# A two-layer Conformer trunk: reading a half bank twice, adding saved sums early, and storing the last tile in halves

## The chip, the cores and the metric

One core of a Trainium2 chip runs the whole program in one launch. The metric is the device time of an execution in microseconds, as the median of several runs.

## What is computed

`x` has 512 positions of 1024 features, in float32. Two layers follow one another, and each has two feed-forward blocks around a mixer:

```python
for l in range(DEPTH):          # DEPTH = 2
    x = x + 0.5 * swiglu(rms_norm(x, ffn1_norm[l]), gate1[l], up1[l], down1[l])
    x = x + mixer(rms_norm(x, mix_norm[l]))      # convolution group and differential attention
    x = x + 0.5 * swiglu(rms_norm(x, ffn2_norm[l]), gate2[l], up2[l], down2[l])

def swiglu(h, w_gate, w_up, w_down):             # 1024 -> 2816 -> 1024
    return (silu(h @ w_gate) * (h @ w_up)) @ w_down
```

## The kernel before

The kernel keeps `x` in SBUF as eight tiles of 128 features by 512 positions. Each product in float32 is made of three products in a shorter format: a weight tile is split into a high and a low part (L100 on ScalarE, L101 on VectorE), the input likewise, and high x high, high x low and low x high are added up in a PSUM bank.

A feed-forward block has 22 tiles of hidden features, and `PARTS` treats them in three groups: six plain ones ("first"), eight ("seven") and eight ("last"). In the groups "seven" and "last" the products are done with seven sub-products in place of eight, in Strassen's manner (Winograd's form): the 1024 inputs are two halves, the 512 positions are two halves of 256, and the two weight tiles that go together make the third pair. The hand-written names show which: `g1`, `g2`, `u1`, `u2` are the four weight blocks, `u2u1`, `g1u1`, `g1u2u1` and `all` sums and differences of them; `b11`, `b21`, `b22` and `t1` to `t4` are the blocks of the input and their sums. A product is a call of `go`: 12 matmuls of 128 x 128 x 256.

Each pair of results has two PSUM banks, each with two halves of 256 columns: `a` and `d` in the first, `b` and `c` in the second. Partial sums that several results need are copied by ScalarE into the SBUF tile `keep` (four quarters of 256) while the bank goes on accumulating.

The up side is `seven` (L396). Its last product, `t3` with `g1u1`, is made by `rest` (L433), which is called late, inside the next pair's products, so that TensorE is not held up. Behind it VectorE makes the two up halves from `a` and two quarters of `keep` (L435, L436), and multiplies them with the gate into the hidden tile (L439). `Hidden.add` (L451) then forms the hidden tile's parts and the sums for the down side (L463 to L473).

The down side is `Pair` (L483), with four pairs for each group: `head` makes the first product and its copy (L509), `body` most of the others with the copies L535 and L539 and the addition "two += keep" (L541), after which the first of the pair's two tiles of `x` is updated (L542). `finish` (L545) makes the last product `t3` and updates the second tile of `x` in three VectorE steps (L548 to L550). It too is called late, inside the body of the next pair, right behind the product with `u2`; for the last pair of a block `tail` calls it.

The weights come by DMA: SP issues the loads into two rings of buffers, `wraw` (five) and `wsum` (four), GpSimd issues loads that add to `wsum`. For each group of down weights, VectorE makes two more sums, L174 (`g1u2u1`) and L175 (`all`); a buffer can be loaded again when the last step that reads it is over, and for that of `g2` L175 is one of these.

The order of the instructions on an engine is chosen by a scheduler with its own timing model; `keep_in_program_order` pins the first matmul of a product and some others. So a change in one helper can move instructions of other lines. In the last block, `store` (L1043) writes a tile of `x` to the output with one DMA of 256 KB on SP's queue when it is done. The last tile is stored by `tail` after the last `finish`.

Of the kernel before, what the change touches and what calls it, by code (L numbers as in the profile page):

```python
# [18 lines left out]
P = 128  # L19
# [50 lines left out]
def trunk(ctx: ExitStack, tc: tile.TileContext, xt, par, lamv, relb, onehot,  # L70
# [325 lines left out]
    def seven(halves, w, banks, fp, before, last):  # L396

        a, d = banks[0][:, :HS], banks[0][:, HS:]  # L400
        b, c = banks[1][:, :HS], banks[1][:, HS:]
        two = banks[1].rearrange("p (n c) -> p n c", n=2)
        keep = fp.tile([P, 4, HS], F32, tag="gn", name="keep", bufs=2)
        g = keep[:, 0::2]

        def go(ps, wt, xt, first=False):


            at = halves.get(xt)
# [12 lines left out]
        S.activation(keep[:, :2], banks[0].rearrange("p (n c) -> p n c", n=2), AF.Copy)  # L422
        go(b, "g2", "b21")
        if not last:
            go(c, "all", "b22")
        go(a, "g1u2u1", "t2")
        saves.append(S.activation(keep[:, 2], a, AF.Copy))
        if last:
            go(c, "all", "b22")
        V.tensor_tensor(two, two, g, op=ALU.add)  # L430
        S.activation(g, two, AF.Silu)

        def rest(out=None):  # L433
            go(a, "g1u1", "t3")
            V.tensor_tensor(d, a, keep[:, 3], op=ALU.add)  # L435
            V.tensor_tensor(a, a, keep[:, 1], op=ALU.add)  # L436
            us = banks[0].rearrange("p (n c) -> p n c", n=2)
            to = us if out is None else out.rearrange("p (n c) -> p n c", n=2)
            V.scalar_tensor_tensor(to, us, -1.0, g, op0=ALU.mult, op1=ALU.mult)  # L439
            return banks[0] if out is None else out  # L440

        return rest

# [39 lines left out]
    class Pair:  # L483
# [25 lines left out]
            self.saved = S.activation(self.keep[:, self.kc], self.c, AF.Copy)  # L509
            return self  # L510

        def body(self, w, before, more=None):
            a, b, c, d, go = self.a, self.b, self.c, self.d, self.go
            both = self.banks[0].rearrange("p (n c) -> p n c", n=2)
            if self.m == 0:
# [14 lines left out]
            else:  # L530
# [3 lines left out]
                go(a, w["g1"], "b11")  # L534
                S.activation(self.keep[:, :2], both, AF.Copy)  # L535
                go(b, w["g2"], "b21")
                go(c, w["all"], "b22")
                go(a, w["g1u2u1"], "t2")
                saves.append(S.activation(self.keep[:, 2], a, AF.Copy))  # L539
            two, xm = self.banks[1].rearrange("p (n c) -> p n c", n=2), x[:, self.m, :]  # L540
            V.tensor_tensor(two, two, self.keep[:, 0::2], op=ALU.add)  # L541
            V.scalar_tensor_tensor(xm, self.banks[1], 0.5, xm, op0=ALU.mult, op1=ALU.add)  # L542
            return nxt

        def finish(self, weight):  # L545
            a, d, xn = self.a, self.d, x[:, self.m2, :]
            self.go(a, weight, "t3")
            V.tensor_tensor(d, a, self.keep[:, self.kc], op=ALU.add)  # L548
            V.tensor_tensor(a, a, self.keep[:, self.kd], op=ALU.add)
            V.scalar_tensor_tensor(xn, self.banks[0], -0.5, xn, op0=ALU.mult, op1=ALU.add)  # L550

    def begin(pr, loads, tail=None):
        ws = [[chunk(src) for src in pair] for pair in loads]
        ps = [pair_banks() for _ in loads]
        return [*zip(ws, ps)], first_products(pr, ws, ps, early=tail is not None, tail=tail)

    def ffn(fp, pr, gu, dn, after, begun, then, spare, aside=None):
        halves = None
        late = []
        jobs = []  # L560
# [29 lines left out]
        for fs, kind in PARTS:  # L590
# [59 lines left out]
            for m in range(KT // 2):  # L650
                m2 = m + KT // 2
                if m == 0:

                    def more(saved):
                        with behind(saved, hid.last[0]):
                            this.split("all", "g1u2u1", "g1u1")

                    with behind(hid.big, hid.sum):
                        ahead[0].split("u2u1")
                    pair = Pair(hid, fp, m, m2).head(this.w["u2u1"])  # L660
                    nxt = pair.body(this.w, lambda: Pair(hid, fp, 1, 1 + KT // 2).head(ahead[0].w["u2u1"]), more)
                else:
                    this = group(after=hid.last if m == 1 else ())
                    pair = nxt if m == 1 else Pair(hid, fp, m, m2).head(this.w["u2u1"])
                    pair.body(this.w, finish)
                if kind == "last":
                    if m:
                        after(m2 - 1)
                    after(m)
                late.append(lambda pair=pair, this=this: pair.finish(this.w["g1u1"]))  # L670

        def tail():
            finish()
            after(KT - 1)

# [357 lines left out]
    for l in range(DEPTH):  # L1033
# [9 lines left out]
        def store(m):  # L1043
            nc.sync.dma_start(out[m], x[:, m, :])

        with tc.tile_pool(name="ffn", bufs=1) as fp:
            begun = ffn(fp, pr, gu1[l], dn1[l], preparing("mix_norm"), begun,
                        lambda tail: begin(nxt["p"], [[wag[l, c, i] for i in range(2)] for c in range(2)], tail),
                        (l == 0, 1), aside if l == 0 else None)
        mixer(l, nxt["p"], preparing("ffn2_norm"), begun)  # L1050
        with tc.tile_pool(name="ffn", bufs=1) as fp:
# [2 lines left out]
                begun = ffn(fp, nxt["p"], gu2[l], dn2[l], preparing("ffn1_norm", l + 1), begun,  # L1054
                            lambda tail: begin(nxt["p"], [[gu1[l + 1, m, i] for i in range(2)] for m in range(2)], tail), (0, 1))
            else:
                ffn(fp, nxt["p"], gu2[l], dn2[l], store, begun, lambda tail: tail(), (0, 0))
        pr = nxt["p"]


# [72 lines left out]
```

## Time and profile before

| | |
|---|---|
| median of three runs | 1779.29 us (1778.25 to 1779.77) |
| the profiled execution | 1778.98 us |
| its span, first to last instruction | 1777.2 us |
| TensorE busy | 1760.0 us (99%) |
| VectorE busy | 1478.7 us (83%) |
| ScalarE busy | 1037.6 us (58%) |
| GpSimd busy | 579.7 us (33%) |
| granted TensorE clock | full, in all 40 slices |

A busy TensorE is one that has a matmul in flight; matmuls overlap, so a busy share near 100% leaves out small gaps. Rows of the timeline give the start, the duration, the engine, the line, the operation, what it writes and reads with the shapes, and in brackets how long the engine was idle before it and what released it. PE is TensorE, DVE is VectorE, ACT is ScalarE, POOL is GpSimd, and SPq is the queue of SyncE, which issues DMAs. Rows of waits give the idle time in total, the number of times and the longest.

### The profile page before, as it was taken

How to read it: one execution, taken by the hardware profiler on the slowest of the kernel's cores; microseconds unless marked ns; L12 is line 12 of the kernel's file. 1: busy time of each engine (PE TensorE's matmuls, PEld its weight loads, DVE VectorE, ACT ScalarE, POOL GpSimd, SP SyncE). 2: the span in 40 equal slices, each digit the busy share in tenths (PEclk: the TensorE clock that was granted, in tenths of full speed). 3: DMA queues.
4: the chain of work that ended last, by engine and by line, in shares of the span. 5: the costliest groups of instructions: out<-in, count | busy, mean ns of one | idle time of the engine just before them, and what ended most of it. 6: DMA issues, size and time to landing. Idle time of an engine off the chain costs nothing.

```text
span 1777.2 us, 32962 instructions
## 1 busy us (share of the span) xinstructions
PE 1760.0 (99%) x11844; PEld 1619.0 (91%) x11844; DVE 1478.7 (83%) x2595; ACT 1037.6 (58%) x1946; POOL 579.7 (33%) x539
## 2 busy tenths in 40 slices
PE   8999999999999999999999999999999999999998
PEld 6799999988788899999988999999887888999998
DVE  7969888968877869889987798899688687698987
ACT  5546566655865436566644565666559554465664
POOL 3011112379972011112310121123798620111122
PEclk9999999999999999999999999999999999999999
DMA  6557677533223446677543577766231334576775
GB/s 215 140 134 184 170 193 188 140 116 101 66 78 107 138 124 175 171 201 177 140 142 107 149 178 178 191 161 174 87 107 49 101 113 125 130 185 168 198 175 125
DMA packets 165317, 257.78 MB, mean 145 GB/s; under 512 B 19127, under 2 KB 60870, under 8 KB 165152
## 3 DMA queue, kind: packets, MB, share of 16 engines
q1 hardware_dynamic: 128448, 201.38, 35.4%
q0 software_dynamic: 36416, 54.12, 18.9%
q8 instruction: 93, 1.52, 0.4%
q14 instruction: 72, 0.59, 0.1%
q10 hardware_dynamic: 288, 0.16, 0.0%
HBM read 253.48 MB, written 3.42 MB: 145 GB/s over the span
## 4 chain that ended last, share of the span: by engine, by line
PE 90%; ACT 3%; DVE 3%; DMA 2%; issue 1%; POOL 1%; SPq 0%; ACTq 0%; DVEq 0%; POOLq 0%
PE ps_pair L413 36%; PE ps_pair L502 14%; PE ps_pair L202 9%; PE ps_pair L203 9%; PE ps_pair L199 9%; PE ps_out L199 2%; PE ps_out L202 2%; PE ps_out L203 2%; PE ps_pair L793 2%; PE ps_pair L792 2%; PE ps_pair L791 2%; DMA wraw<-in_dn 1%; ACT whi L100 1%; PE ps_sc L908 0%; DVE actl L292 0%
## 5 line engine op out<-in xcount | busy, mean ns | idle before, releaser
L100 ACT ACTIVATE whi<-wraw 128x512 fp32r<-128x512 f32 x752 | 457.4, 627 | 406.8 <-PE ps_pair L202 160.5
L101 DVE TENSOR_TENSOR wlo<-wraw,whi 128x512 fp32r<-128x512 f32 x648 | 440.2, 699 | 110.2 <-ACT whi L100 96.5
L159 POOL DMA_DIRECT2D wsum<-in_gu x128 | 112.3, 915 | 711.1 <-DMA wsum<-in_gu 295.5
L413 PE MATMUL ps_pair<-acth,wlo 128*128 128x256 f32 x1024 | 289.8, 283 | 0.0
L413 PE MATMUL ps_pair<-actl,whi 128*128 128x256 f32 x1024 | 289.8, 283 | 0.0
L413 PE MATMUL ps_pair<-acth,whi 128*128 128x256 f32 x1024 | 289.8, 283 | 0.0
L413 PE MATMUL ps_pair<-th,whi 128*128 128x256 f32 x768 | 217.3, 283 | 0.0
L413 PE MATMUL ps_pair<-tl,whi 128*128 128x256 f32 x768 | 217.3, 283 | 0.0
L413 PE MATMUL ps_pair<-th,wlo 128*128 128x256 f32 x768 | 217.3, 283 | 0.0
L199 PE MATMUL ps_pair<-acth,whi 128*128 128x512 f32 x512 | 200.1, 395 | 5.8 <-ACT whi L100 5.8
L202 PE MATMUL ps_pair<-actl,whi 128*128 128x512 f32 x512 | 200.6, 393 | 0.4 <-DVE actl L292 0.3
L203 PE MATMUL ps_pair<-acth,wlo 128*128 128x512 f32 x512 | 199.4, 391 | 0.0
L413 PEld LDWEIGHTS ps_pair<-acth,whi 128*128 128x128 f32 x1024 | 196.6, 192 | 0.2
L413 PEld LDWEIGHTS ps_pair<-actl,whi 128*128 128x128 f32 x1024 | 196.6, 192 | 0.2
L413 PEld LDWEIGHTS ps_pair<-acth,wlo 128*128 128x128 f32 x1024 | 196.6, 192 | 0.0
L159 POOL DMA_DIRECT2D wsum<-in_dn x112 | 98.9, 1138 | 268.6 <-DVE wlo L101 50.2
L413 PEld LDWEIGHTS ps_pair<-th,whi 128*128 128x128 f32 x768 | 147.5, 192 | 0.0
L413 PEld LDWEIGHTS ps_pair<-tl,whi 128*128 128x128 f32 x768 | 147.5, 192 | 0.0
L413 PEld LDWEIGHTS ps_pair<-th,wlo 128*128 128x128 f32 x768 | 147.5, 192 | 0.0
L101 POOL TENSOR_TENSOR wlo<-wraw,whi 128x512 fp32r<-128x512 f32 x104 | 137.1, 1339 | 26.4 <-ACT whi L100 20.5
L502 PE MATMUL ps_pair<-hh,whi 128*128 128x256 f32 x512 | 144.9, 283 | 0.0
L502 PE MATMUL ps_pair<-hl,whi 128*128 128x256 f32 x512 | 144.9, 283 | 0.0
(201 smaller groups left out, 4495.1 us busy)
## 6 DMA issues: line engine op xcount, KB each, us to landing
wraw<-in_gu SPq DMA_DIRECT2D x288, 256.0 KB, 3.5
wsum<-in_gu SPq DMA_DIRECT2D x128, 256.0 KB, 3.8
wsum<-in_gu POOLq DMA_DIRECT2D x128, 256.0 KB, 4.8
wraw<-in_dn SPq DMA_DIRECT2D x68, 256.0 KB, 3.0
wraw<-in_wqkv SPq DMA_DIRECT2D x48, 256.0 KB, 2.6
wraw<-in_wout SPq DMA_DIRECT2D x48, 256.0 KB, 2.6
wraw<-in_dn SPq DMA_DIRECT2D x64, 128.0 KB, 3.8
wraw<-in_wag SPq DMA_DIRECT2D x32, 256.0 KB, 2.8
```

Of the source, the lines that this page charges most:

```text
L100: S.activation(hi, raw, AF.Copy)
L101: (eng or V).tensor_tensor(out=lo, in0=raw, in1=f32(hi), op=ALU.subtract)
L159: nc.gpsimd.dma_start(dst[:, to], src, accum_op=ALU.add)
L199: first = T.matmul(ps, wh, xh, start=start, stop=False)
L202: T.matmul(ps, wh, xl, start=False, stop=False)
L203: T.matmul(ps, wl, xh, start=False, stop=stop)
L413: mm = T.matmul(ps, l, r, start=first and i == j == 0, stop=False, skip_group_check=True)
L502: mm = T.matmul(ps, s[:, f], r, start=side not in self.begun, stop=False, skip_group_check=True)
L791: T.matmul(ps[n], xh[:, t], wh, start=k == 0, stop=False)
L792: T.matmul(ps[n], xh[:, t], wl, start=False, stop=False)
L793: T.matmul(ps[n], xl[:, t], wh, start=False, stop=k == KT - 1)
```

## The change

There are four edits. In `rest`, one addition reads `a` twice, once for each quarter of `keep`, and writes both up halves to the hidden tile; the multiplication with the gate then works on the hidden tile in place. In `finish`, the two saved quarters are added to the tile of `x` before the last product (in one instruction where the quarters lie in the right order, in two where they do not), and behind the product `a` is added to both halves by one instruction that reads it twice. In the body of the last pair of the last block, the product with `all` comes after that with `g1u2u1`. The last tile of `x` is finished and stored in two halves, the first on SP's queue and the second on ScalarE's.

```diff
-        def rest(out=None):
+        def rest(out):
             go(a, "g1u1", "t3")
-            V.tensor_tensor(d, a, keep[:, 3], op=ALU.add)
-            V.tensor_tensor(a, a, keep[:, 1], op=ALU.add)
-            us = banks[0].rearrange("p (n c) -> p n c", n=2)
-            to = us if out is None else out.rearrange("p (n c) -> p n c", n=2)
-            V.scalar_tensor_tensor(to, us, -1.0, g, op0=ALU.mult, op1=ALU.mult)
-            return banks[0] if out is None else out
+            to = out.rearrange("p (n c) -> p n c", n=2)
+            V.tensor_tensor(to, a.unsqueeze(1).broadcast_to([P, 2, HS]), keep[:, 1::2], op=ALU.add)
+            V.scalar_tensor_tensor(to, to, -1.0, g, op0=ALU.mult, op1=ALU.mult)
+            return out
...
-        def body(self, w, before, more=None):
+        def body(self, w, before, more=None, last=False):
...
                 go(b, w["g2"], "b21")
-                go(c, w["all"], "b22")
+                if not last:
+                    go(c, w["all"], "b22")
                 go(a, w["g1u2u1"], "t2")
                 saves.append(S.activation(self.keep[:, 2], a, AF.Copy))
+                if last:
+                    go(c, w["all"], "b22")
...
-        def finish(self, weight):
-            a, d, xn = self.a, self.d, x[:, self.m2, :]
+        def finish(self, weight, store=None):
+            a, xn = self.a, x[:, self.m2, :]
+            xs = xn.rearrange("p (n c) -> p n c", n=2)
+            if self.kd < self.kc:
+                V.scalar_tensor_tensor(xs, self.keep[:, 1::2], -0.5, xs, op0=ALU.mult, op1=ALU.add)
+            else:
+                for n, k in ((0, self.kd), (1, self.kc)):
+                    V.scalar_tensor_tensor(xs[:, n], self.keep[:, k], -0.5, xs[:, n], op0=ALU.mult, op1=ALU.add)
             self.go(a, weight, "t3")
-            V.tensor_tensor(d, a, self.keep[:, self.kc], op=ALU.add)
-            V.tensor_tensor(a, a, self.keep[:, self.kd], op=ALU.add)
-            V.scalar_tensor_tensor(xn, self.banks[0], -0.5, xn, op0=ALU.mult, op1=ALU.add)
+            if store is None:
+                V.scalar_tensor_tensor(
+                    xs, a.unsqueeze(1).broadcast_to([P, 2, HS]), -0.5, xs, op0=ALU.mult, op1=ALU.add)
+            else:
+                for n, queue in enumerate((nc.sync, nc.scalar)):
+                    V.scalar_tensor_tensor(xs[:, n], a, -0.5, xs[:, n], op0=ALU.mult, op1=ALU.add)
+                    store(n, xs[:, n], queue)
...
-                    pair.body(this.w, finish)
+                    pair.body(this.w, finish, last=kind == "last" and end and m == KT // 2 - 1)
...
-        def tail():
+        def tail(halves=None):
+            if halves:
+                late.clear()
+                pair.finish(this.w["g1u1"], halves)
+                return
             finish()
             after(KT - 1)
...
+        def store_half(n, half, queue):
+            queue.dma_start(out[KT - 1][:, n * HS : (n + 1) * HS], half)
...
-                ffn(fp, nxt["p"], gu2[l], dn2[l], store, begun, lambda tail: tail(), (0, 0))
+                ffn(fp, nxt["p"], gu2[l], dn2[l], store, begun, lambda tail: tail(store_half), (0, 0), end=True)
```

In the new file the addition and the multiplication of `rest` are L436 and L437; in `body` the copies are L533 and L538, the addition is L542 and the update of the first tile L543; in `finish` the early sums are L550 (one instruction) or L553 (two), the step behind the product is L556, and the two halves of the last tile are L560. L100, L101, L174, L175, L292 and L300 keep their numbers.

More of the change, by code (lines that the diff above doesn't have):

```diff
@@ L555, in begin, with ffn @@
         return [*zip(ws, ps)], first_products(pr, ws, ps, early=tail is not None, tail=tail)
-    def ffn(fp, pr, gu, dn, after, begun, then, spare, aside=None):
+    def ffn(fp, pr, gu, dn, after, begun, then, spare, aside=None, end=False):
         halves = None
```

## The prediction

> **What bounds the kernel now.** I read the page first, then who waits for whom on the TensorE, then the timeline of the last eight microseconds, then the places where a down pass loses time.
>
> ```profile
> span 1777.2 us, 32962 instructions
> PE 1760.0 (99%) x11844; PEld 1619.0 (91%) x11844; DVE 1478.7 (83%) x2595; ACT 1037.6 (58%) x1946; POOL 579.7 (33%) x539
> ...
> PE ps_pair L502 <- ACT keep L535: 2.5, 5, 0.9
> PE ps_o L938 <- ACT at L931: 1.7, 4, 0.5
> PE ps_pair L502 <- ACT keep L539: 0.5, 1, 0.5
> ```
>
> TensorE is busy for 1760.0 of 1777.2 us, and what it waits for inside the feed-forward layers is small: five times for L535 (2.5 us in all) and once for L539 (0.5 us). So work taken off VectorE, which is busy 83%, is worth nothing by itself. The time can move in three places only: behind TensorE's last matmul, in the waits of the down passes, and in the mixers, where TensorE is not at its rate.
>
> The end, from the timeline (start, duration, engine, line, operation):
>
> ```profile
> 1769.97 0.28 PE L502 MATMUL ps_pair<-yh,wlo 128*128 128x256 f32 x1
> ...
> 1770.29 0.38 ACT L539 ACTIVATE keep<-ps_pair 128x256 f32<-128x256 f32 x1 [3.72 <-PE ps_pair L502]
> 1770.70 0.70 DVE L541 TENSOR_TENSOR ps_pair<-ps_pair,keep 128x512 f32<-128x512 f32 x1 [4.54 <-ACT keep L539]
> 1770.72 0.38 PE L502 MATMUL ps_pair<-yh,whi 128*128 128x256 f32 x1 [0.47 <-ACT keep L539]
> ...
> 1771.44 0.69 DVE L542 SCALAR_TENSOR_TENSOR x<-ps_pair,x 128x512 f32<-128x512 f32 x1
> ...
> 1772.13 0.28 PE L502 MATMUL ps_pair<-yh,wlo 128*128 128x256 f32 x1
> 1772.16 2.27 SPq L1044 DMA_DIRECT2D out<-x  x2
> 1772.45 0.43 DVE L548 TENSOR_TENSOR ps_pair<-ps_pair,keep 128x256 f32<-128x256 f32 x1 [0.32 <-PE ps_pair L502]
> 1772.91 0.43 DVE L549 TENSOR_TENSOR ps_pair<-ps_pair,keep 128x256 f32<-128x256 f32 x1
> 1773.38 0.69 DVE L550 SCALAR_TENSOR_TENSOR x<-ps_pair,x 128x512 f32<-128x512 f32 x1
> ...
> out<-x SPq DMA_DIRECT2D x8, 256.0 KB, 2.1
> ```
>
> TensorE stalls once more before the last product, three VectorE steps follow its last matmul, and then one store of 256 KB, issued at 1774.1 (the two stores of the L1044 row end at 1774.43 and one takes 0.34), lands in about 2.1 us.
>
> **Part 1: up halves (64 times).** L435, L436 and L439 become one addition that reads the bank half twice and one multiplication out of SBUF. Old: 0.43 + 0.43 + 0.69 = 1.55 us, the first two as L548 and L549 above, the third as L550. No row shows a read that repeats a half; its output has 512 elements like L541 (0.70), and its input 256 like L548 (0.43), so it costs 0.43 to 1.13 (an estimate: both rows added), and I take 0.70. The multiplication out of SBUF:
>
> ```profile
> L463 DVE TENSOR_TENSOR hl<-hid,hh x64: 680/685/687, 127.0 to 1733.4; 128x512 fp32r<-128x512 f32 x64
> L175 DVE TENSOR_TENSOR wraw<-wraw x96: 674/683/2307, 97.6 to 1760.7; 128x512 f32<-128x512 f32 x96
> ```
>
> 0.69 as well, so the pair saves 0.16 us, 64 times 10 us of VectorE (at worst it adds 0.27 each). TensorE hides this: none of its waits names L435 to L439. The bank is also released one step after the product instead of three; TensorE has no wait for it, so that too is worth 0. The Trainium skill, "SBUF — State Buffer", on contention says that VectorE and GpSimd share one port pair and that the loser is blocked for a whole instruction. The 2307 ns of L175 agree, but the 64 L463 in the same stretches never pass 687 ns.
>
> **Part 2: down's copied sums (32 times).** L548, L549 and L550 (1.54 us) become a step out of SBUF (L550 of the new file, ahead of the product; in each pass's first pair, two of 256 elements at L553) and one of 512 elements behind it. VectorE saves 0.15 us each, again hidden. What matters is the order that the scheduler makes of it. In the built order of the changed kernel, the second group of every down pass now has L175 behind the addition "two += keep" (L542 there, L541 here), which waits for ACT. Ahead of L174 lie the new L556 and L550, about 0.69 each, where L548 and L549 (0.43 each) lay, so L174 comes some 0.5 later too; that is still ahead of the addition's wait. Before, in the last pass and in a pass in the middle (VectorE, then GpSimd):
>
> ```profile
> 1748.06 0.69 DVE L550 SCALAR_TENSOR_TENSOR x<-ps_pair,x 128x512 f32<-128x512 f32 x1
> 1748.66 0.68 DVE L175 TENSOR_TENSOR wraw<-wraw 128x512 f32<-128x512 f32 x1
> 1749.67 0.70 DVE L541 TENSOR_TENSOR ps_pair<-ps_pair,keep 128x512 f32<-128x512 f32 x1 [0.33 <-ACT keep L539]
> ...
> 329.62 0.70 DVE L541 TENSOR_TENSOR ps_pair<-ps_pair,keep 128x512 f32<-128x512 f32 x1 [0.27 <-ACT keep L539]
> 330.23 0.75 DVE L292 SCALAR_TENSOR_TENSOR actl<-x,par,acth 128x512 fp32r<-128x512 f32 x1
> 330.90 1.86 DVE L175 TENSOR_TENSOR wraw<-wraw 128x512 f32<-128x512 f32 x1
> ...
> 330.81 1.40 POOL L300 TENSOR_TENSOR ssum<-ssum,sq 128x512 f32<-128x512 f32 x1
> ```
>
> L175 frees the buffer into which SP loads g2 of the group after next. In five passes (the four of PARTS "seven" and the final one) it moves from 1748.66 to 1749.67 + 0.60 (the pitch between the first two rows) = 1750.27, 1.61 us later. Queued behind it are that load, ACT's splits of it, and behind those on ACT the copy L535, for which TensorE waits:
>
> ```profile
> 1749.73 6.29 DMA wraw<-in_dn
> ...
> 1757.84 0.58 ACT L535 ACTIVATE keep<-ps_pair 128x512 f32<-128x512 f32 x1
> ...
> 1757.58 0.28 PE L502 MATMUL ps_pair<-hh,wlo 128*128 128x256 f32 x1
> 1758.47 0.39 PE L502 MATMUL ps_pair<-yh,whi 128*128 128x256 f32 x1 [0.62 <-ACT keep L535]
> ...
> 1628.24 7.14 DMA wraw<-in_dn
> ...
> wraw<-in_dn SPq DMA_DIRECT2D x68, 256.0 KB, 3.0
> ```
>
> These loads take 6.29 and 7.14 us where the median is 3.0, so over half of it is a queue of other transfers; a load that is issued 1.61 later into the same queue lands between 0 and 1.61 later, and I take 0.7 (3.0 of 6.7 is the part that moves with it). The other four passes, L535 and TensorE's next start:
>
> ```profile
> 214.99 0.58 ACT L535 ACTIVATE keep<-ps_pair 128x512 f32<-128x512 f32 x1
> 754.00 0.58 ACT L535 ACTIVATE keep<-ps_pair 128x512 f32<-128x512 f32 x1
> 1095.76 0.58 ACT L535 ACTIVATE keep<-ps_pair 128x512 f32<-128x512 f32 x1
> 1636.00 0.58 ACT L535 ACTIVATE keep<-ps_pair 128x512 f32<-128x512 f32 x1
> ...
> 216.69 0.28 PE L502 MATMUL ps_pair<-yh,whi 128*128 128x256 f32 x1
> 754.89 0.28 PE L502 MATMUL ps_pair<-yh,whi 128*128 128x256 f32 x1
> 1097.58 0.28 PE L502 MATMUL ps_pair<-yh,whi 128*128 128x256 f32 x1
> 1636.64 0.39 PE L502 MATMUL ps_pair<-yh,whi 128*128 128x256 f32 x1 [0.22 <-ACT keep L535]
> ```
>
> Room is start less end of L535, less 0.05: 1.07, 0.26, 1.19 and none. With 0.7 later: 0 + 0.44 + 0 + 0.6 (its delay is a little shorter) = +1.05; with the full delay 0.54 + 1.35 + 0.42 + 1.34 = +3.65; with none 0. In the final pass TensorE starts at 1758.47 what was due at 1757.58 + 0.12 (its pitch): 0.77 lost. There the same delay is partly made good, because one store of 256 KB leaves that queue: the built order puts it ahead of this group's loads. I take +0.2, between -0.77 and +1.61. The three passes in the middle go the other way: L175, which at 330.90 came behind L541 and L292, now comes directly behind the addition, 0.67 earlier (its 1.86 us stand beside GpSimd's L300). But ACT gets one more step, L291, ahead of the copy, about 0.6 like L535's 0.58. I take -0.1 for each, -0.3; the bounds are -1.8 (1.66 is left of the first row's 2.5 after 0.62 and 0.22, and a restart costs some hundredths more each) and +1.8 (the ACT step alone, three times).
>
> **Part 3: the last pair.** With the "all" product between t2 and t3, the copy L539 runs beside 12 matmuls and TensorE's stall goes: the last product starts at 1769.97 + 0.12 instead of 1770.72, and its last matmul at 1771.41 instead of 1772.13: 0.72 saved. What is late next is VectorE: "two += keep" now waits for the end of "all" (1769.97 + 0.32 = 1770.29), and its successor ends 0.74 + 0.69 later, at 1771.72; the product's result is there at 1771.41 + 0.32 = 1771.73. A tie, at no cost. The two halves then take 0.43 each and end at 1772.16 and about 1772.6 instead of 1774.07. The second half's store is issued near 1772.65 instead of 1774.1: 1.45 saved. Two halves and the store ahead of them now come within 0.9 us (SP needs 0.34 for each issue, the ACT queue is empty). How fast stores move, in slices of 0.75 us from 1748:
>
> ```profile
> GB/s 146 66 270 215 107 125 85 178 292 271 241 211 79 0 0 0 0 0 319 30 0 106 243 0 0 254 96 0 0 0 0 22 0 273 77 27 322 11 0 0
> ```
>
> The last store moves in about one slice (322 GB/s), so a half could land 0.4 sooner, or wait 0.4 behind the two others: 1.05 to 1.85 saved. I price its landing like the whole's, 2.1, the only row of a store: 1.45. The Trainium skill, "DMA: Bandwidth & Descriptors", on the two cost components, gives about 2.0 us fixed and bytes at 436 GB/s: an estimate from it is 2.6 us for the whole and 2.3 for a half, so halving would bring 0.3 and this part 1.75. The same page says that queues of several engines only save issue time. The whole store's 2.1 is already under that 2.6.
>
> **Part 4: mixers.** No line of theirs changes, but the built order of TensorE, VectorE and GpSimd does. The longest of their waits on TensorE, L938 above, has 1.7 us in all; the reordering could remove or double it: I take 0, bounds -1.7 and +1.7.
>
> **Sum.** -1.45 + 1.05 + 0.2 - 0.3 + 0 = -0.5 us. The profiled execution took 1778.98 us (span 1777.2 and 1.78 around it), so 1778.48; it lay 0.31 under the median of three, 1779.29, so the forecast for a median is 1778.8. A measurement of this kernel can tell about 0.2% (3.56 us) from no change.
>
> **Rivals.**
> 1. *The g2 load sets the pace (slower).* If its landing follows its issue, part 2 costs 3.65 + 1.61, the rest -1.45: +3.8, 1783.1. It decides once L535 starts over 1.1 us later in "seven". For it: L175 names the chain that ended last at 1749.73. Against: over half of the load's time is queue. Chance 0.13, of which 0.09 past 0.2%.
> 2. *The waits go.* Earlier bank releases, one store moved off the queue and lighter VectorE clear all L535 stalls: -1.45 - 1.8 - 0.77 - 0.4 = -4.4, 1774.9. Against: L175 is put later. Chance 0.13, of which 0.11 past 0.2%.
> 3. *The end brings nothing*: three stores at once, or VectorE late before the last halves: 1.45 shrinks to 0.4, and with part 2 as summed the median is 1779.8. Chance 0.14.
>
> The forecast, a gain of half a microsecond with mixers of either sign, has 0.60 and a range of its own of 1776.5 to 1781. Faster by over 0.2%: 0.12, slower 0.10, within 0.78. The range leaves out a tenth on each side: 1775.4 to 1782.4.
>
> **What would show it.** L543 of the new file ending within 0.1 us of the last matmul's end, no wait for L538 at the end, the last store issued 1.4 us earlier relative to the first matmul of "all"; L175 behind L542 in each "seven" pass and L533 there 0.5 to 1 us later; waits for L533 between 2 and 5 us in all. Wrong would be: waits for L533 of over 6 us or none, a mixer longer by over 2 us, or TensorE waiting for a bank.

## The result and the profile after

The changed kernel takes 1782.32 us (median of 15 runs, 1780.42 to 1785.60) beside 1779.29 us for the kernel before in the same rounds: a ratio of 1.0016, 95% interval 1.0009 to 1.0024. It is slower by about 3 us, inside the bound of 0.2% that the prediction had set for "no change", but above its own range of 1776.5 to 1781, and slower where half a microsecond was to be gained. The profiled execution took 1782.02 us, with a span of 1779.1 us.

From the page of the changed kernel, the span and the busy shares:

```profile
span 1779.1 us, 32890 instructions
...
PE 1761.6 (99%) x11844; PEld 1620.8 (91%) x11844; DVE 1475.1 (83%) x2508; ACT 1041.6 (59%) x1946; POOL 577.1 (32%) x539
```

VectorE has 87 instructions fewer and is busy 3.6 us less, and yet the span is 1.9 us longer. Who waits for whom on TensorE (us in total, times, longest):

```profile
PE ps_pair L199 <- ACT whi L100: 5.9, 1, 5.9
PE ps_pair L500 <- ACT keep L533: 4.7, 7, 1.6
PE ps_out L202 <- DVE actl L908: 1.0, 2, 0.5
PE ps_out L199 <- DVE x L1030: 0.9, 4, 0.2
```

The waits for the copy of `body` (now L533) have grown from 2.5 us in five places to 4.7 us in seven; those for the last copy (L539 before, L538 now) are gone. The first row is the start of the program, which every kernel here has.

Rows from the last microseconds in the timeline of the changed kernel:

```profile
1768.88 6.89 SPq L1059 DMA_DIRECT2D out<-x  x2
...
1773.60 0.28 PE L500 MATMUL ps_pair<-hh,wlo 128*128 128x256 f32 x1
1773.72 0.28 PE L500 MATMUL ps_pair<-yh,whi 128*128 128x256 f32 x1
1773.99 0.70 DVE L542 TENSOR_TENSOR ps_pair<-ps_pair,keep 128x512 f32<-128x512 f32 x1 [3.07 <-PE ps_pair L500]
1774.73 0.69 DVE L543 SCALAR_TENSOR_TENSOR x<-ps_pair,x 128x512 f32<-128x512 f32 x1
1775.04 0.28 PE L500 MATMUL ps_pair<-yh,wlo 128*128 128x256 f32 x1
1775.36 0.75 DVE L560 SCALAR_TENSOR_TENSOR x<-ps_pair,x 128x256 f32<-128x256 f32 x2
1775.87 0.38 SPq L1062 DMA_DIRECT2D out<-x  x1
1776.15 0.35 ACTq L1062 DMA_DIRECT2D out<-x  x1
```

The last product starts 0.12 us behind the one before it, the 0.72 us of stall are gone, and L543 ends at 1775.42, within 0.1 of the end of the last matmul at 1775.32. From the start of the last matmul to the end of the span it is 4.06 us now and was 5.07 (1772.13 to 1777.2). So the end gave 1.7 us (0.72 of stall and 1.0 behind the last matmul), and something else took 3.6.

To find it, I set the starts of the same matmuls in both traces side by side, stage by stage. At the last matmul the changed kernel is 2.91 us late: 2.22 were lost in three down passes, 1.16 in the two mixers and 0.60 in the first 120 us (a difference that the runs of other kernels show with either sign); 1.07 were gained in the last "seven" pass of layer 1 and in the final pass. The three passes are the "last" groups whose tiles of `x` are normalised for the block that follows (the prediction called them the three in the middle; below they are the norm passes). Besides the down side's own work they hold L291, L299 (ScalarE), L292 (VectorE) and L300 (GpSimd) for each finished tile. Cut out from first to last down matmul, they look like this. First before, then after. Each row gives the window, its length, the busy time and instructions of PE, PEld (the loading of weights into TensorE), DVE, ACT and POOL, then the granted clock (1.00 is full), the busy share of the DMA engines and GB/s:

```profile
310.29:354.33 44.04, 43.57 (x351) 42.67 (x350) 42.48 (x67) 30.09 (x59) 16.24 (x15) 1.00 0.54 137
848.49:892.97 44.48, 43.58 (x350) 42.68 (x349) 42.91 (x67) 30.11 (x59) 16.52 (x15) 1.00 0.53 137
1191.18:1235.18 44.00, 43.58 (x351) 42.69 (x349) 42.44 (x67) 29.80 (x58) 16.34 (x15) 1.00 0.54 140
sum 132.52, PE 130.72 PEld 128.04 DVE 127.83 ACT 90.01 POOL 49.09; mean PE 43.58 PEld 42.68 DVE 42.61 ACT 30.00 POOL 16.36
```

```profile
310.88:356.20 45.32, 43.57 (x350) 42.67 (x349) 44.07 (x64) 30.29 (x59) 16.86 (x15) 1.00 0.51 131
851.20:895.48 44.28, 43.56 (x350) 42.67 (x349) 43.03 (x64) 30.17 (x59) 17.04 (x15) 1.00 0.53 133
1193.70:1238.84 45.14, 43.57 (x350) 42.67 (x349) 43.89 (x64) 30.19 (x59) 16.92 (x15) 1.00 0.52 136
sum 134.74, PE 130.70 PEld 128.01 DVE 131.00 ACT 90.65 POOL 50.82; mean PE 43.57 PEld 42.67 DVE 43.67 ACT 30.22 POOL 16.94
```

This is the view that the prediction lacked. VectorE, 83% busy over the span, is busy 127.83 of 132.52 us here, 96%. And with fewer instructions it is busier after the change. The second of the three passes is 0.2 us shorter after the change, the first and the third are 1.28 and 1.14 longer. The timeline of the first norm pass after the change, VectorE and then GpSimd, shows what keeps VectorE busy:

```profile
330.01 2.21 DVE L292 SCALAR_TENSOR_TENSOR actl<-x,par,acth 128x512 fp32r<-128x512 f32 x1
332.15 0.69 DVE L542 TENSOR_TENSOR ps_pair<-ps_pair,keep 128x512 f32<-128x512 f32 x1
332.75 1.16 DVE L175 TENSOR_TENSOR wraw<-wraw 128x512 f32<-128x512 f32 x1
...
338.22 1.75 DVE L292 SCALAR_TENSOR_TENSOR actl<-x,par,acth 128x512 fp32r<-128x512 f32 x1
...
341.10 1.78 DVE L174 TENSOR_TENSOR wraw<-wsum,wraw 128x512 f32<-128x512 f32 x1
...
349.60 1.77 DVE L292 SCALAR_TENSOR_TENSOR actl<-x,par,acth 128x512 fp32r<-128x512 f32 x1
...
330.39 2.95 POOL L300 TENSOR_TENSOR ssum<-ssum,sq 128x512 f32<-128x512 f32 x1
337.93 1.50 POOL L300 TENSOR_TENSOR ssum<-ssum,sq 128x512 f32<-128x512 f32 x1 [4.58 <-ACT sq L299]
340.58 1.75 POOL L300 TENSOR_TENSOR ssum<-ssum,sq 128x512 f32<-128x512 f32 x1 [1.16 <-ACT sq L299]
349.04 1.78 POOL L300 TENSOR_TENSOR ssum<-ssum,sq 128x512 f32<-128x512 f32 x1 [6.71 <-ACT sq L299]
```

Steps that take 0.68 to 0.75 us elsewhere take 1.16 to 2.21 in these rows, where an L300 of GpSimd runs beside them; most take some 1.1 us more. Added up over all VectorE steps that start inside the three windows and take over 0.2 us more than the shortest step of their kind in the kernel, it is 14.2 us before (15 steps) and 17.5 us after (18 steps).

### The profile page after: what moved, and what is told of

It is laid out like the page before. It is cut to its first block, busy times and chain, and to the rows that moved or that the text cites. A ratio compares the mean times of both kernels' runs of the same rounds, so it can differ in the third digit from the quotient of the medians.

```text
span 1779.1 us, 32890 instructions
## 1 busy us (share of the span) xinstructions
PE 1761.6 (99%) x11844; PEld 1620.8 (91%) x11844; DVE 1475.1 (83%) x2508; ACT 1041.6 (59%) x1946; POOL 577.1 (32%) x539
## 4 chain that ended last, share of the span: by engine, by line
PE 91%; DVE 5%; ACT 3%; issue 1%; DMA 1%; DVEq 0%; ACTq 0%; POOL 0%
PE ps_pair L413 36%; PE ps_pair L500 13%; PE ps_pair L202 9%; PE ps_pair L199 9%; PE ps_pair L203 9%; PE ps_pair L808 2%; PE ps_pair L807 2%; PE ps_pair L806 2%; PE ps_out L202 1%; PE ps_out L203 1%; PE ps_out L199 1%; PE ps_sc L923 1%; DVE wlo L101 1%; ACT whi L100 1%; PE ps_v L838 1%
## 5 line engine op out<-in xcount | busy, mean ns | idle before, releaser
L100 ACT ACTIVATE whi<-wraw 128x512 fp32r<-128x512 f32 x752 | 458.1, 627 | 413.0 <-PE ps_pair L202 163.8
L101 DVE TENSOR_TENSOR wlo<-wraw,whi 128x512 fp32r<-128x512 f32 x648 | 446.9, 708 | 108.2 <-ACT whi L100 102.1
L101 POOL TENSOR_TENSOR wlo<-wraw,whi 128x512 fp32r<-128x512 f32 x104 | 134.0, 1305 | 37.2 <-ACT whi L100 31.2
```

Source lines behind the costliest of these rows:

```text
L100: S.activation(hi, raw, AF.Copy)
L101: (eng or V).tensor_tensor(out=lo, in0=raw, in1=f32(hi), op=ALU.subtract)
```

## The experiments

Each kernel was timed in rounds with the kernel before, and the ratio is to that. "Norm passes" is the sum over the three passes cut out in the same way, from one profile of each kernel:

| kernel | median us | ratio, 95% interval | norm passes us |
|---|---|---|---|
| before | 1779.3 to 1779.9 | | 132.5 |
| after | 1782.32 | 1.0016 (1.0009 to 1.0024) | 134.7 |
| up_only | 1777.97 | 0.9990 (0.9982 to 0.9999) | 131.4 |
| sums_only | 1786.27 | 1.0042 (1.0029 to 1.0055) | 139.4 |
| tail_only | 1778.22 | 0.9992 (0.9983 to 1.0001) | 133.4 |
| copy_first | 1783.66 | 1.0020 (1.0011 to 1.0029) | 136.0 |
| up_tail | 1776.50 | 0.9983 (0.9974 to 0.9992) | 132.4 |
| sums_not_norm | 1774.68 | 0.9972 (0.9962 to 0.9983) | 131.9 |
| sums_norm_only | 1781.11 | 1.0008 (0.9999 to 1.0017) | 135.2 |
| short_l300 | 1777.68 | 0.9989 (0.9980 to 0.9998) | 130.3 |
| sum_first | 1782.21 | 1.0018 (1.0009 to 1.0027) | 136.2 |
| short_before | 1775.72 | 0.9980 (0.9971 to 0.9989) | 129.2 |
| sums_late | 1779.70 | 1.0003 (0.9994 to 1.0012) | 135.4 |
| sq_vector | 1781.19 | 1.0007 (0.9998 to 1.0016) | 136.0 |
| sq_vector_old | 1772.49 | 0.9956 (0.9943 to 0.9968) | 129.3 |
| sum_first_vector | 1774.26 | 0.9969 (0.9957 to 0.9981) | 129.8 |

### The parts one by one: up_only, sums_only, tail_only

```diff
 up_only: before, and in rest
+            V.tensor_tensor(to, a.unsqueeze(1).broadcast_to([P, 2, HS]), keep[:, 1::2], op=ALU.add)
+            V.scalar_tensor_tensor(to, to, -1.0, g, op0=ALU.mult, op1=ALU.mult)
 sums_only: before, and in finish, ahead of the product and behind it
+                V.scalar_tensor_tensor(xs, self.keep[:, 1::2], -0.5, xs, op0=ALU.mult, op1=ALU.add)
+            self.go(a, weight, "t3")
+                V.scalar_tensor_tensor(
+                    xs, a.unsqueeze(1).broadcast_to([P, 2, HS]), -0.5, xs, op0=ALU.mult, op1=ALU.add)
 tail_only: before, and for the last pair "all" behind t2, its sums early, its tile stored in halves
```

> The kernel before with the up halves' edit alone (one addition that reads the bank half twice, one multiplication out of SBUF). Theory M (the loss is made in the three feed-forward passes whose results go to a norm, where L292 beside GpSimd's L300 delays L175, and one more L291 delays the copy that TensorE waits for): in this kernel's built order the copy stands ahead of the second L291 as before, and L292 stands behind L175 instead of ahead of it, so the three waits there shrink below the 0.4, 0.9 and 0.35 us of before: median 0.5 to 2 us under the kernel before. Theory B (the doubled read or SBUF operand is dear): VectorE's addition over 0.9 us and a median 1 to 3 us over. Theory X (the mixers' new order costs): a mixer longer by 0.3 to 0.9 us each and a median about 1 us over.

> The kernel before with the early sums alone (saved quarters added to x ahead of the last product, one step behind it); the end is neither swapped nor halved. Theory M: the built order of these three passes has L292 ahead of L175 and two pairs of L291 and L299 ahead of the copy, so the waits for the copy there are as long as after the change or longer, 1.5 to 2.5 us in each of two or three passes: median 3 to 5 us over the kernel before. Theory G (the later g2 load in the seven passes): waits in those passes of 0.5 to 1.4 us. Theory X: mixers 0.3 to 0.9 us longer each and no change in the passes.

> The kernel before with the last pair's swap, its finish with early sums and its two half stores; all other pairs as before. All theories: the order elsewhere is the old one, the wait for L539 goes and the last store is issued 1.45 us earlier: median 1.0 to 1.9 us under the kernel before, and the waits for L535 as before (about 2.5 us in all). If the run-to-run spread rather than the passes makes the difference, it is within 0.5 us of the kernel before.

The up edit alone gains 1.8 us by its ratio (0.2 to 3.2), the end alone 1.4 (3.0 gained to 0.2 lost), the early sums alone lose 7.5 (5.2 to 9.8). The loss is the early sums', most of it in the norm passes (139.4 us for 132.5). The four "seven" passes of sums_only lose 1.9 us, where those of the kernel before lose 0.5. In sums_only TensorE waits for the copy nine times:

```profile
PE ps_pair L502 <- ACT keep L535: 9.3, 9, 3.0
```

### Which passes: up_tail, sums_not_norm, sums_norm_only

```diff
 up_tail: after, in finish
+            if store is None:
+                ... the old finish
 sums_not_norm: after, in finish (self.late is set in the three norm passes)
+            if self.late:
+                ... the old finish
 sums_norm_only: the same, self.late set in all passes but the norm passes and the final one
```

> The up halves' edit and the last pair's edits together, with the old finish in all other pairs: the change without its early sums. If the parts add up (1.4 and 1.1 us under the kernel before when alone): 1776.3 to 1777.5 us, 2 to 3 under the kernel before, the fastest so far. If the two gains are one and the same: 1777.5 to 1778.5.

> The changed kernel with the old finish in the three passes whose results go to a norm; early sums stay in the four passes of PARTS seven and in the final one, whose built order is that of the changed kernel. Theory M (the loss is made in the three norm passes): within 0.7 us of the kernel without early sums, 1776.3 to 1777.7. Theory G (the loss is the later g2 load in the other passes, or early sums cost wherever they are): 1.5 to 4 us over it.

> The reverse: early sums in the three norm passes and the final one, the old finish in the passes of PARTS seven. Theory M: as slow as the changed kernel, 1781.3 to 1783.3. Theory G: 1.5 to 4 us faster than it.

With the old finish in the norm passes alone, the change becomes a gain of 5.0 us (0.9972, 0.9962 to 0.9983) and the norm passes fall from 134.7 to 131.9. With the early sums there and nowhere else but in the final pass, they take 135.2. So the "seven" passes, on which the prediction spent a term of +1.05, are not where the loss of the changed kernel is. The norm passes are where the edit costs, but their own length is only a part of it: in the profile of sums_not_norm (1776.65 us, the longest of its seven executions) the two mixers are shorter than in the changed kernel too, by 2.7 us, nearly as much as the norm passes, and no line of the mixers differs between the two.

### A first theory, and its fall: copy_first, short_l300, sum_first, short_before, sums_late

In the second stretch of a norm pass, the built order of VectorE was the addition, L292, L175 before and is L292, the addition, L175 after; on ScalarE an L291 has come ahead of the copy L533. My first theory was that this order costs it. copy_first puts the norm steps of each pair's second tile behind the copy:

```diff
-                        after(m2 - 1)
+                        with behind(pair.copied):
+                            after(m2 - 1)
```

> The changed kernel with the norm's steps for the second of a pair's tiles ordered behind the copy L533, so that no extra L291 stands ahead of it; L292 still stands ahead of L175 in the second group. Theory M: about 0.6 us less in each of three passes: median 1.5 to 2 us under the changed kernel, so 0.5 to 1.5 over the kernel before. Theories B, G and X: no gain, 2.5 to 3.5 over.

It gained nothing. The waits for the copy fell to 3.5 us, and new ones came behind them, of the next stage's first products for VectorE's splits:

```profile
PE ps_pair L500 <- ACT keep L533: 3.5, 5, 1.8
PE ps_pair L203 <- DVE wlo L101: 2.6, 6, 0.7
```

short_l300 leaves the order alone and shortens GpSimd's addition to 16 of 512 columns. It leaves out the rest of the sums of squares, so its result is not that of the program, and it is read for its time alone (`x_done` is set once the first norm of the program is over, and `ffn2_norm` is the norm behind the mixer, so both conditions together leave the norm passes):

```diff
-                G.tensor_tensor(self.s, self.s, sq, op=ALU.add)
+                n = 16 if self.gain != "ffn2_norm" and x_done else SEQ
+                G.tensor_tensor(self.s[:, :n], self.s[:, :n], sq[:, :n], op=ALU.add)
```

> The changed kernel, with GpSimd's addition L300 in the norm passes made over 16 of 512 columns, so that the sums of squares there are incomplete; the built order of VectorE and ScalarE is that of the changed kernel. Theory P (a VectorE step with two SBUF operands is held up while L300 runs, and L292, L174 and L175 on the way to the copy are the ones hit): L292 and L175 fall from up to 2.2 us to about 0.75, the waits for L533 in the norm passes fall from 1.7 to at most 0.6 us each, median 1.5 to 3.5 us under the changed kernel (1778.8 to 1780.8). Theory O (the order alone makes the loss): within 0.7 us of the changed kernel.

It takes 4.6 us off the changed kernel's median. No VectorE step in the norm passes is drawn out by over 0.2 us any more, where 17.5 us in all had been:

```profile
sum 130.32, PE 129.74 PEld 127.86 DVE 121.14 ACT 94.40 POOL 35.51; mean PE 43.25 PEld 42.62 DVE 40.38 ACT 31.47 POOL 11.84
```

That showed what the blocking is worth in this kernel, not that it explains the difference between two kernels. Three runs asked that:

```diff
 sum_first: after, with the fifth tile's norm steps issued behind the third group's L175
+                    if m == 2 and kind == "last" and not end:
+                        with behind(this.summed):
+                            after(KT // 2)
...
 short_before: before, with the same short L300
 sums_late: after, in finish
+            if store is None:
+                self.go(a, weight, "t3")
+                ... the step that reads a twice
             ... the step that adds keep
```

> The changed kernel, with the fifth tile of the three norm passes (L292 and its neighbours) issued behind the third group's sum 'all' (L175). In the built order L175 then comes directly behind L542 and ahead of L292, as the prediction had assumed; on ScalarE the copy L533 comes ahead of L291, as in copy_first. Theory 'L292 ahead of L175, drawn out beside GpSimd's L300, makes the splits and the copy late': the three norm passes lose 2 us less than in the changed kernel (2.2) and 3 less than in copy_first (3.5); the time is 1780.0 (1779 to 1781). Rival 'the early sums and the other order around them cost it, wherever L175 stands': it stays with the changed kernel or copy_first, 1782.3 to 1783.7.

> The kernel before, with GpSimd's L300 in the three norm passes over 16 of 512 columns (the sums of squares are incomplete). Instruction order as before. Theory 'the changed kernel loses in the norm passes because more of VectorE's chain stands beside L300': the kernel before gains less from this than the 4.6 us that the changed kernel gained; with the norm passes equal in both, what is left of their difference is 0.3, so 1778.0 (1777 to 1779), a gain of 1.3 (0.3 to 2.3). Rival 'L300 draws out both kernels alike, and the loss has another cause': the same 4.6 us gain, 1774.7.

> The changed kernel, with the step that adds the saved quarters to x (L550, L553) put behind the product's step and not ahead of the product; the last pair as in the changed kernel. The built order in the second stretch of a norm pass is still L292, the addition, L175, but ScalarE's copy comes ahead of L291. Theory 'the place of L292 ahead of L175 costs it': the norm passes still lose about 1.5 us in all, and the time is 1781 (1780 to 1783). Rival 'the early step in front of the product costs it': the loss goes, and the time is that of the kernel with the up edit and the tail alone, 1776.5 (1775.5 to 1777.5).

sum_first has the order that the prediction had assumed, and takes 1782.21 us, as the changed kernel does: the theory of the one order fell. The stall of 1.73 us at 339.97 is gone in its trace, but the norm passes are longer (136.2), because the lost time comes back later, as in copy_first:

```profile
PE ps_pair L500 <- ACT keep L533: 3.5, 5, 1.1
PE ps_pair L203 <- DVE wlo L101: 2.6, 6, 0.7
```

As long as L300 draws VectorE's steps out (all 15 of them in sum_first are steps of L101 or L292, 1.0 to 1.1 us each), neither of these two orders shortens the norm passes. sums_late lies between its two expectations: the norm passes are as long as ever (135.4) although the step stands behind the product, and what it regains is in the mixers (1.1 us under before, where the changed kernel is 1.2 over). And short_before, which leaves out the same part of the sums of squares, gained 3.6 us where 1.3 or 4.6 had been expected. Its norm passes run at 129.2, with no TensorE wait left in them:

```profile
sum 129.18, PE 129.18 PEld 127.71 DVE 121.87 ACT 91.39 POOL 31.97; mean PE 43.06 PEld 42.57 DVE 40.62 ACT 30.46 POOL 10.66
```

So GpSimd's additions hold up both kernels, and the changed one by a microsecond or so more: between the short kernels the norm passes differ by 1.1 us, between the full ones by 2.2. The other half of the 2.2 us stays when L300 is short, so the blocking is not all of it.

### Two causes, taken away singly and together: sq_vector, sq_vector_old, sum_first_vector

L300 goes to VectorE in the norm passes, which takes GpSimd's blocking away and adds 0.60 us a time to VectorE's own work (L301 in the new files). Inside the three windows that is 15 additions, 9 us; the two expectations below reckon with 18, and with 19.6 and 15.3 us of drawn-out steps where 17.5 and 14.0 lie inside the windows:

```diff
-                G.tensor_tensor(self.s, self.s, sq, op=ALU.add)
+                eng = V if self.gain != "ffn2_norm" and x_done else G
+                eng.tensor_tensor(self.s, self.s, sq, op=ALU.add)
 sq_vector: after;  sq_vector_old: sums_not_norm;  sum_first_vector: sum_first
```

> The changed kernel, with L300 of the three norm passes on VectorE instead of GpSimd; the result is complete. Theory 'VectorE sets the length of a norm pass, and each L300 on GpSimd blocks one of its steps for about 1.09 us': in the changed kernel the steps of VectorE in the three passes are drawn out by 19.6 us in all, in place of which come 18 steps at a pitch of 0.60, 10.8 us; the passes lose most of the 4.6 us that the shortened L300 took away: 1778.5 (1777 to 1780). Rival 'the drawn-out steps lie in time that VectorE would idle in anyway': 18 more steps on an engine that is 97% busy in these passes make them 5 to 10 us longer: 1787 (1785 to 1792).

> sums_not_norm (the old finish in the norm passes), with L300 of the three norm passes on VectorE; the result is complete. Theory 'blocking by GpSimd': its VectorE steps are drawn out by 15.3 us in the three passes, against 10.8 us of added steps; the passes take 131.9 us where TensorE alone needs 129.2, so at most 2.7 can go: 1773.5 (1772 to 1775). Rival 'the drawn-out steps cost nothing': 18 more steps on VectorE, 1779 (1777 to 1784).

sq_vector_old does what the theory of blocking expects and a little more: 1772.49 us, 0.9956 (0.9943 to 0.9968), with no wait for the copy in a norm pass. sq_vector doesn't: it stands between the two expectations, and its norm passes take 136.0 us without any blocking. Their sums, first of sq_vector, then of sq_vector_old:

```profile
sum 136.03, PE 130.84 PEld 127.92 DVE 128.49 ACT 91.45 POOL 26.52; mean PE 43.61 PEld 42.64 DVE 42.83 ACT 30.48 POOL 8.84
```

```profile
sum 129.31, PE 129.31 PEld 127.76 DVE 124.45 ACT 90.89 POOL 26.54; mean PE 43.10 PEld 42.59 DVE 41.48 ACT 30.30 POOL 8.85
```

VectorE's share does not tell the two apart: it is busy 94% of the norm passes in sq_vector and 96% in sq_vector_old, which loses next to nothing. So there is a second cause, the order. ScalarE's timeline ahead of the same copy (L534 in sq_vector, L535 in sq_vector_old) shows one side of it; first sq_vector, with TensorE's next start:

```profile
335.67 0.71 ACT L291 ACTIVATE acth<-x,par 128x512 fp32r<-128x512 f32 x1
336.28 0.61 ACT L299 ACTIVATE sq<-x 128x512 f32<-128x512 f32 x1
336.81 0.71 ACT L291 ACTIVATE acth<-x,par 128x512 fp32r<-128x512 f32 x1
337.42 0.61 ACT L299 ACTIVATE sq<-x 128x512 f32<-128x512 f32 x1
337.94 0.57 ACT L534 ACTIVATE keep<-ps_pair 128x512 f32<-128x512 f32 x1
...
338.56 0.39 PE L501 MATMUL ps_pair<-yh,whi 128*128 128x256 f32 x1 [0.63 <-ACT keep L534]
```

```profile
333.56 0.71 ACT L291 ACTIVATE acth<-x,par 128x512 fp32r<-128x512 f32 x1
334.17 0.61 ACT L299 ACTIVATE sq<-x 128x512 f32<-128x512 f32 x1
334.69 1.14 ACT L100 ACTIVATE whi<-wraw 128x512 fp32r<-128x512 f32 x2
335.74 0.57 ACT L535 ACTIVATE keep<-ps_pair 128x512 f32<-128x512 f32 x1
```

In sq_vector the scheduler puts the norm steps of two tiles, 2.3 us, ahead of the copy for which TensorE waits; in sq_vector_old, those of one. The other side is on VectorE: in sq_vector an L292 and the moved addition stand ahead of L543 (the addition "two += keep") and of L175, and ScalarE's splits start 21.7 us into the first norm pass, where they start at 20.7 in sq_vector_old. The last run takes GpSimd's additions away, mends the order by the edit of sum_first, and leaves the early sums in:

> sum_first (the changed kernel with the fifth tile's norm steps behind L175, and so the copy L533 ahead of most of them) with L300 of the norm passes on VectorE as in sq_vector. Theory 'two causes, each enough to hold a pass up: GpSimd's additions block VectorE, and norm steps stand ahead of the copy for which TensorE waits': with both gone the three norm passes come from 136.2 us to within 1.5 of the 129.3 us that TensorE needs, and the time is 1776 (1774.5 to 1777.5). Rival 'a third cause in the early sums themselves': the passes stay over 133 us, and the time is 1780 or more.

```profile
sum 129.81, PE 129.43 PEld 127.75 DVE 125.36 ACT 91.80 POOL 26.51; mean PE 43.14 PEld 42.58 DVE 41.79 ACT 30.60 POOL 8.84
```

129.8 us, against 136.2 in sum_first and 136.0 in sq_vector, and 1774.26 us in all: the edit to the order gains 6.2 us once the additions are on VectorE, the move of the additions gains 6.4 once the order is mended, and neither shortens the changed kernel's passes (134.7) without the other. With both, the passes are 0.5 us from those of sq_vector_old. Two limits belong to this. sq_vector does not take the blocking away and nothing else, since it also adds 9 us to VectorE; in short_l300, without that work, the changed kernel's order costs at most 1.1 us (130.3 for 129.2). And the edit moves steps on both engines (three norm steps still stand ahead of the copy on ScalarE, for four in sq_vector), so no run tells which of the two counts.

The profile of sum_first_vector, its longest execution of six (1776.12 us), lost 4.1 us in a "seven" pass, where the loads of `wsum` were late. TensorE stood still for 2.33 us ahead of 1105.27, and then the granted clock fell for some 3.4 us and the matmuls came every 0.21 us instead of every 0.12:

```profile
1106.00:1110.00 4.00, 4.00 (x24) 4.00 (x23) 3.47 (x6) 1.18 (x3) 0.86 (x1) 0.57 0.93 191
```

sq_vector_old is the fastest version found, 7.3 us under the kernel before; whether the kernel before would gain as much by its L300 alone wasn't run.

## Why the prediction was wrong

**The failed steps.** The first is in the opening part: "work taken off VectorE, which is busy 83%, is worth nothing by itself". 83% is a mean over the span. In the norm passes it is 96%, and there VectorE's time counts: with the steps no longer drawn out, the kernel before gains 3.3 us in these passes and 3.6 in all (short_before). The share alone decides nothing, though: sq_vector_old has the same 96% there and loses 0.1 us. The second is the term of -0.3 for the three passes in the middle, within bounds of -1.8 and +1.8: their part is +2.2 in the profile. It was worked out from the place of one step, "L175 ... now comes directly behind the addition, 0.67 earlier". In the trace L175 follows the addition, at 332.75, but an L292 drawn out to 2.21 us stands ahead of both. ScalarE's splits wait for L175; first before, then after:

```profile
332.80 0.63 ACT L100 ACTIVATE whi<-wraw 128x512 fp32r<-128x512 f32 x1 [1.71 <-DVE wraw L175]
333.94 0.63 ACT L100 ACTIVATE whi<-wraw 128x512 fp32r<-128x512 f32 x1 [2.26 <-DVE wraw L175]
```

Counted from the first matmul of the pass (310.29 and 310.88), that is 22.51 and 23.06 us: 0.55 later, not 0.67 earlier. The L291 ahead of the copy was seen and priced at 0.6 for each pass, which is about right: the two together are the 1.16 us by which the stall behind this copy grew (0.57 to 1.73). In the second norm pass, where L292 met no L300 (0.74 us at 870.33), the stall behind the same copy is 0.65 us shorter than before, and the pass is not longer.

The third is in part 1, where a rule of the Trainium skill was weighed. The Trainium skill, "SBUF — State Buffer", in the section "SBUF: two separate sides", says that VectorE and GpSimd lock a shared port pair for a whole instruction, and that a VectorE step with two SBUF inputs is among those that need it. I set against it that the 64 L463 "in the same stretches" never pass 687 ns. The trace agrees with that page: in the norm passes after the change 18 steps with two SBUF inputs (L101, L174, L175, L292) took 0.3 to 1.5 us more beside an L300, most of them 1.0 to 1.1, while those with an operand in PSUM (L542, L543, L556) never passed 0.70 there. And the L463 are not in the same stretches: none of the 64 runs beside an L300. In one place the trace goes further than a loser that waits: at 330.01 both steps are drawn out, L292 to 2.21 and L300 to 2.95 us, and the rows do not show which held up which. The change takes two PSUM steps of 0.43 out of every pair and puts one SBUF step of 0.68 in; before, part of an L300 could run beside the PSUM steps, and two L292 of the first norm pass lost only 0.43 and 0.82 us (they took 1.17 and 1.56, where the undisturbed one takes 0.74). The second of them, from the kernel before:

```profile
347.13 0.42 DVE L549 TENSOR_TENSOR ps_pair<-ps_pair,keep 128x256 f32<-128x256 f32 x1
347.46 1.56 DVE L292 SCALAR_TENSOR_TENSOR actl<-x,par,acth 128x512 fp32r<-128x512 f32 x1
347.19 1.29 POOL L300 TENSOR_TENSOR ssum<-ssum,sq 128x512 f32<-128x512 f32 x1 [5.91 <-ACT sq L299]
```

That these steps are what covered L300 is an argument from the trace; no run changed the place of an operand alone.

**Part 2, "seven" and final.** The +1.05 for the four "seven" passes did not come: they are 0.4 us shorter together, and no TensorE wait is left in them, where one place that lost 0.38 was before. L175 stands behind L542 and starts 1.61 us later in the first three of them, as foretold to the hundredth, but the copy behind it moved by +0.55, -0.78, +0.25 and -0.42 us, where +0.7 had been taken: in this profile the delay did not reach it. The mechanism is not refuted by that. In sums_only, with the same place of L175, the copy comes 0.94, 0.74, 1.89 and 0.08 us later and three of the four passes wait for it. With one profile of each kernel, what spared the changed kernel is open. The rival in which that load sets the pace was not met in the changed kernel, nor was the rival in which the waits go (4.7 us of them, in the range of 2 to 5 that the prediction had named). The final pass lost 0.84 in the same place as 0.77 before, for +0.2 foretold.

**Part 1** otherwise: L436 and L437 take 0.69 and 0.68 us, for 0.70 and 0.69. That this is worth nothing was wrong: up_only gains 1.8 us (0.2 to 3.2). Its norm passes are 1.1 us shorter and its mixers 1.6. Only one pair of L436 and L437 lies in each norm pass, so the 0.16 saved there is not the reason. What differs is the order: L175 stands ahead of L292 in the first norm pass and starts 19.9 us into it, where it started at 20.6 before. That this order makes the gain was expected before the run, but no run isolates it.

**Part 3.** Right, and a little under-sized: 1.7 us in the profile for 1.45. The tie was one (L543 ends 0.1 us after the last matmul). The last store is issued 1.11 us behind the start of the last matmul, where it was 1.97, and a half lands in 1.9 to 2.0 us, where the whole took 2.1: halving brought 0.1 there, not the 0.3 of that part's second estimate, so it is by other terms that the 1.7 comes near its 1.75. tail_only gives 1.4, with an interval that reaches zero. The rival in which the end brings nothing fell by the profile.

**Part 4.** Mixers were put at 0 with bounds of 1.7; they took 1.16 us more, a further term that failed, though inside its bounds. Which order of theirs costs that stays open: by one profile of each, the kernels with the up edit and the old finish in the norm passes lie 1.5 to 2.2 us under before, sums_late and sum_first_vector 1.1 and 1.6 under, while short_l300 and sums_norm_only stay 1.1 over. No run changed a mixer alone.

**The sum.** In the profile: -1.7 for the end, +2.2 for the norm passes, +1.2 for the mixers, -0.4 for the "seven" passes and +0.6 at the start, +1.9 in all, for -0.5. The +0.6 at the start is of the size by which other kernels differ there either way.

## What to carry to other kernels

Read the busy share stage by stage before calling an engine's work free: an engine that is 83% busy over the span can be 96% busy in the stage that sets the time. Then look at what that time is made of, since a share of 96% went with a loss of 3.3 us in one kernel here and of 0.1 in another: count for each step where its operands lie and what runs on GpSimd beside it, and which steps stand ahead of the one that the bottleneck waits for. And where a stall goes away by reordering, look for it one stage later before counting the gain.

## What the runs showed of the hardware

One L300 on GpSimd, 1.29 us long when alone, cost a VectorE step with two SBUF inputs 1.0 to 1.1 us in 12 of 18 places in the changed kernel and in all 15 of sum_first, and up to 2.5 in sums_late; L300 itself grew to as much as 2.97 us beside them in the changed kernel. The same addition takes 0.68 us on VectorE, at a pitch of 0.60. Giving it to VectorE, busy 96% of these passes as it was, shortened them from 131.9 to 129.3 us (sums_not_norm to sq_vector_old, with medians of 1774.68 and 1772.49).

After a TensorE stall of 2.33 us the granted clock fell to half for 3.4 us in sum_first_vector; after one of 2.98 us in sums_only it did not.
